# Keys and values of a second cross attention: made during the mix and kept in DRAM

## The chip, the core and the metric

The kernel runs on one core of a Trainium2 chip. The metric is the device time of one execution in microseconds (us), the median over several runs. The profile is one further execution, recorded by the hardware profiler.

## The reference, cut to what matters

Two transformer blocks run one after the other on 512 tokens of width 1024. The second block has a mix of three recurrent branches with gates, an attention over a memory of 256 rows, and a feed-forward network. The keys and values of that attention depend on the memory and on weights alone, not on the tokens.

```python
def second_block(x, mem, ...):
    mem_n = rms_norm_2(mem, norm_mem)
    h = rms_norm_2(x, norm_mix[l])
    p_rw, p_s5, p_gla, p_gate = _split_2(h @ w_in[l], IN_SIZES)
    y_rw, y_s5, y_gla = rwkv7_mix(p_rw, ...), s5_mix(p_s5, ...), gla_mix(p_gla, ...)
    gates = jax.nn.sigmoid(p_gate).reshape(B, L, N_BRANCH, D_MODEL)
    merged = (gates[:, :, 0] * (y_rw @ w_branch[l, 0])
              + gates[:, :, 1] * (y_s5 @ w_branch[l, 1])
              + gates[:, :, 2] * (y_gla @ w_branch[l, 2]))
    x = x + merged @ w_out[l]
    x = x + cross_attention(rms_norm_2(x, norm_xattn[l]), mem_n, xa_wq[l], xa_wkv[l], xa_wo[l])
    x = x + conv_ffn(rms_norm_2(x, norm_ffn[l]), ffn_w_up[l], ...)

def cross_attention(h, mem_n, wq, wkv, wo):          # 4 heads of 256
    q = (h @ wq).reshape(B, L, XA_HEADS, XA_HEAD)
    kv = (mem_n @ wkv).reshape(B, M, 2, XA_HEADS, XA_HEAD)
    k, v = kv[:, :, 0], kv[:, :, 1]
    s = jnp.einsum('bqhd,bkhd->bhqk', q, k) * (XA_HEAD ** -0.5)
    o = jnp.einsum('bhqk,bkhd->bqhd', softmax(s), v).reshape(B, L, D_MODEL)
    return o @ wo
```

## The kernel before, in words

Every matrix product is made of three matmuls, so that two rounded halves of each operand (`hi` and `lo`) stand for one float32 number: high by high (L282), high by low (L283), low by high (L284), in `mm3`. A weight tile of 128x512 (256 KB) is loaded through SP's queue (L310), rounded on ScalarE (L312) and its remainder taken on VectorE (L314); `split` and `split_scaled` do the same for data (L245, L264). A product that is 512 tokens wide issues matmuls of 512 columns, one over the 256 rows of the memory matmuls of 256.

The program is one instruction stream for each engine, in the order in which the Python code emits it. Around a chain of dependent work (a recurrence, an attention) the code emits pieces of other jobs as filler. `kit.push` puts a job (a generator) on a list with a kind; `kit.fill(us)` emits pieces of the jobs that are ready until a counted amount of TensorE work is emitted, kinds 0 and 1 by turns, and within a kind in the order in which they were pushed; `kit.need` emits a job to its end; `kit.flush` emits all that is left. A negative yield in a job says that nothing more of it is due for that long. The filler is thus placed by counted work, not by what happens on the chip.

Buffers of 128x512 come from three tags `a`, `b`, `c`, whose sizes `kit.room` sets. A string of four letters says which tag the streams take: stream 0 the main chain, 1 the jobs of kind 0, 2 the jobs of kind 1, 3 those of kind 2. In the mix it is `"abcc"` with 22, 11 and 21 tiles; `kit.flow(SFLOW)` makes it `"accc"` for the attention.

The second block's part that the change touches, with the times that the profile shows:

- From 1562 to 2111 us the **mix** (`mix`, L2218). The main chain is the rwkv recurrence (`kit.fill(20.0)`, `rwkv`): its preparation (1562 to 1656), the inversion of its small triangular matrices on VectorE (1656 to 1741), then four passes over the chunks (1741 to 1854, 1854 to 1947, 1947 to 2034, 2034 to 2111). The jobs of kind 0 beside it are the low-rank projections (`rwkv_lora`), the gates (`gates_g(b)`, L2182: 192 matmuls of 512 columns, 8 gate tiles each) and the merges of the branches (`merge_g`, L2196). The jobs of kind 1 are the branches S5 and then GLA (`branch1`, `branch2`), of which each pushes its merge and the next gates behind it. `kit.flush` ends it (to 2121).
- 2121 to 2144: `merge_g(0)`, the rwkv branch's output weights, which also makes the operand `O`.
- 2144 to 2198: the product with `w_out` (192 matmuls of 512 columns), with `kit.fill(3, 10)` ahead of each quarter. The filler there is `memory()` (L2253): it loads the memory, splits it and makes its norm (`mr`, `mrb`).
- 2198 to 2362: `cross` (L2281). Head 0's keys and values (`keys`, `vals`) and query are made first, then four heads run in `kit.attention`, which emits 4.5 us of filler at each step: the queries, keys and values of heads 1 to 3 and half of the output product. All keys and values together are 384 matmuls of 256 columns, the queries and the output 384 of 512.
- 2362 to the end: the feed-forward network and the last norm.

Of the kernel before, what the change touches and what calls it, by code (L numbers as in the profile page):

```python
# [10 lines left out]
F32 = mybir.dt.float32  # L11
F32R = mybir.dt.float32r
AF = mybir.ActivationFunctionType
ALU = mybir.AluOpType
# [3 lines left out]
S = 512  # L18
D = 1024
DT = D // 128  # L20
MEM = 256
# [14 lines left out]
BOTH = {"mm": "mm ch si", "si": "si", "ch": "ch"}  # L36
X_BOTH = {"mm": "mm ch", "si": "si", "ch": "mm ch"}
LATE = {"mm": "mm", "si": "si", "ch": "ch", "tr": "ch"}, dict(mm=3, ch=3, si=2)
SFLOW = "accc"
AB_FILL, CD_FILL, X_FILL = (0.9, 1.2), (1.15, 1.3, 1.1), (1.1, 1.4)  # L40


# [607 lines left out]
def tok(b):  # L650
    return lambda a: a[:, b * 128 : b * 128 + 128]
# [3 lines left out]
DENSE_K = [(j * 128, 128, [0, 1, 2, 3]) for j in range(4)]  # L655
# [664 lines left out]
class Second:  # L1320
# [899 lines left out]
    def mix(self):  # L2220
        kit, I = self.kit, self.I
        self.xs = kit.xs
        self.merged, self.gates, self.O = {}, {}, []
        gla, s5 = [], []

        def branch1():
            yield from self.s5_g(s5, lambda: kit.push(branch2(), kind=1))
            kit.push(self.merge_g(1, s5, g1))
            self.g2 = kit.push(self.gates_g(2))

        def branch2():
            yield from self.gla_g(gla)
            kit.push(self.merge_g(2, gla, self.g2))
            self.g0 = kit.push(self.gates_g(0))

        kit.push(branch1(), kind=1)
        lora = kit.push(self.rwkv_lora())
        g1 = kit.push(self.gates_g(1))
        kit.fill(20.0)
        kit.need(lora)  # L2240
        rw = self.rwkv()
        kit.flush()
        kit.run(self.merge_g(0, rw, self.g0))
        job = kit.push(self.memory(), kind=2, stream=1)
        for c in range(4):
            kit.fill(3, 10)
            kit.run(kit.proj_g(I["w_out"][c], self.O, lambda i, p: self.add(2 * c + i, p, "norm_xattn")))
        kit.need(job)


    def memory(self):

        kit, nc, I = self.kit, self.nc, self.I  # L2253
        ms = self.ms = []
        mems = [kit.load("", src=src) for src in I["mem2T"]]
        yield -6
        for m in range(DT):
            if m % 2 == 0:
                mem, hl = mems[m // 2], kit.u()
            c = slice(m % 2 * MEM, m % 2 * MEM + MEM)  # L2260
            ms.append([z[:, c] for z in hl])
            kit.split_scaled(mem[:, c], self.vec("norm_mem", m), *ms[m])
            if m == 0:
                acc = kit.f(MEM)
                nc.scalar.square(acc, mem[:, c])
            else:
                sq = kit.f(MEM)
                nc.scalar.square(sq, mem[:, c])
                nc.gpsimd.tensor_tensor(acc, acc, sq, op=ALU.add)
            yield -1  # L2270
        self.mr = kit.t([128, 2], "mr2", 1)
        nc.vector.tensor_copy(self.mr, kit.rpow(kit.sums(acc, kit.ones, [tok(0), tok(1)]), 1.0 / D, EPS))
        big = kit.spread_begin(self.mr, 2)
        yield -4
        self.mrb = kit.spread_end(big)

    def cross(self):
        kit, nc, I = self.kit, self.nc, self.I
        xs, ms, mr, mrb = kit.xs, self.ms, self.mr, self.mrb
        st, O = {}, {}  # L2280
        sc = kit.small(4, "scq")  # L2281

        def keys(h):
            def emit(j, p):
                if not j:
                    hl = kit.u()
                    st["k", h] = [[z[:, j * MEM : j * MEM + MEM] for z in hl] for j in range(2)]
                f = kit.f(MEM)
                nc.vector.tensor_tensor(f, p, mrb, op=ALU.mult)
                kit.split(f, *st["k", h][j])  # L2290

            yield from kit.proj_g(I["xa_wk"][h], ms, emit)

        def vals(h):
            st["v", h] = []

            def emit(b, p):
                st["v", h].append(kit.u(256))
                kit.split_scaled(p, mr[:, b : b + 1], *st["v", h][b])

            yield from kit.proj_tok_g(I["xa_wv"][h], ms, [tok(0), tok(1)], emit)

        def query(h):
            st["q", h] = []

            def emit(j, p):
                st["q", h].append(kit.u())
                if not h and not j:
                    nc.vector.tensor_scalar(sc, kit.rstd(), 256.0**-0.5, None, op0=ALU.mult)
                kit.split(p, *st["q", h][j])  # L2310

            yield from kit.proj_g(I["xa_wq"][h], xs, emit)

        def out(ts, g=None):
            for t in ts:
                if isinstance(O[t], list):
                    kit.need(O[t])
            for c in range(4):
                w = I["xa_wo"][c][:, :, ts[0] : ts[-1] + 1]
                yield from kit.proj_g(w, [O[t] for t in ts], lambda i, p: self.add(2 * c + i, p, g))  # L2320

        def done(h, sums):
            s = []

            def end():
                big = kit.inverse(sums)
                yield -2
                rb = kit.spread_end(big)
                for j in range(2):
                    nc.vector.tensor_tensor(s[j], s[j], rb, op=ALU.mult)  # L2330
                    hl = kit.u()
                    kit.split(s[j], *hl)
                    O[2 * h + j] = hl

            def f(outs):
                for j in range(2):
                    s.append(kit.f())
                    nc.scalar.copy(s[j], outs[j])
                O[2 * h] = O[2 * h + 1] = kit.push(end(), True)
                if h == 1:  # L2340
                    kit.push(out(range(0, 4)))

            return f

        kit.run(keys(0))
        kit.run(vals(0))
        kit.run(query(0))
        jobs = [[]] + [[kit.push(g(h)) for g in (query, keys, vals)] for h in range(1, 4)]

        def heads():  # L2350
            for h in range(4):
                kit.need(*jobs[h])
                qk = []
                for (qh, ql), (kh, kl) in zip(st["q", h], st["k", h]):
                    qk += [(qh, kh), (qh, kl), (ql, kh)]
                sums = kit.small(4, "sums")
                soft = kit.soft_full(sc, [sums[:, b : b + 1] for b in range(4)])
                yield Head(kit, qk, st["v", h], [(0, 256)] * 4, DENSE_K[:2], soft, done(h, sums), 4.5)

        kit.attention(heads())  # L2360
        kit.flush()
        kit.run(out(range(4, 8), "norm_ffn"))
# [94 lines left out]
def program(tc, ctx, I, out):  # L2457
    kit = Kit(tc, ctx, I)
    f = First(kit)
    kit.banks(*APART)  # L2460
    kit.room("abbb", a=26, b=31)
    V, P = kit.nc.vector, kit.nc.gpsimd
    f.begin()
    kit.by(P)
    f.mixer_ab()
    kit.by(V)
    kit.share(X_BOTH)
    f.cross(0)
    kit.share(BOTH)
    kit.room("aaaa", a=50)  # L2470
    f.ffn(0, f.g_mix[1])
    kit.share(APART[0])
    kit.by(V, P)
    kit.room("abbb", a=24, b=33)
    f.mixer_cd()
    kit.by(V)
    kit.share(X_BOTH)
    f.cross(1)
    kit.banks(*LATE)
    kit.room("abbb", a=31, b=50-31)  # L2480
    s = Second(kit)
    take, done = handover(kit, f, s)
    job = kit.push(s.s5_make_g())
    f.ffn(1, take)
    kit.need(job)
    done()
    kit.room("abcc", a=22, b=11, c=54-22-11)
    s.reset = kit.load("reset")
    s.mix()
    kit.flow(SFLOW)  # L2490
    s.cross()
    kit.room("aaaa", a=50)
    s.ffn()
    s.finish(out)
# [13 lines left out]
```

## Time and profile before

| | |
|---|---|
| median of 3 runs | 2738.64 us (2735.85 to 2743.93) |
| the profiled execution | 2742.08 us, its span in the trace 2740.3 us |
| TensorE matmul busy | 2630.8 us, 96% of the span |
| VectorE, ScalarE, GpSimd busy | 1594.6, 1182.4 and 519.7 us |
| mean granted TensorE clock | 0.968 of full speed |
| HBM read and written | 234.04 and 22.15 MB, 93 GB/s over the span |

The times from 1562 us on are those of the trace, counted from the start of the span. PE is TensorE's matmuls, PEld its weight loads, DVE VectorE, ACT ScalarE, POOL GpSimd, and SP the engine that issues most transfers. A matmul's busy time in the profile is not its pace: matmuls overlap, and the pace is read from the distance of two starts. PEclk is the granted TensorE clock as a share of full speed (2.4 GHz); its other level is one half.

### The profile page before, as it was taken

How to read it: one execution, taken by the hardware profiler on the slowest of the kernel's cores; microseconds unless marked ns; L12 is line 12 of the kernel's file. 1: busy time of each engine (PE TensorE's matmuls, PEld its weight loads, DVE VectorE, ACT ScalarE, POOL GpSimd, SP SyncE). 2: the span in 40 equal slices, each digit the busy share in tenths (PEclk: the TensorE clock that was granted, in tenths of full speed). 3: DMA queues.
4: the chain of work that ended last, by engine and by line, in shares of the span. 5: the costliest groups of instructions: out<-in, count | busy, mean ns of one | idle time of the engine just before them, and what ended most of it. 6: DMA issues, size and time to landing. Idle time of an engine off the chain costs nothing. (4 is left out here: it accounts for less than half of the span.)

```text
span 2740.3 us, 37093 instructions
## 1 busy us (share of the span) xinstructions
PE 2630.8 (96%) x13432; PEld 2124.6 (78%) x13432; DVE 1594.6 (58%) x3076; ACT 1182.4 (43%) x2209; POOL 519.7 (19%) x439
## 2 busy tenths in 40 slices
PE   8999999999999998999999889799999999999998
PEld 6668778888776787887877667677878788888886
DVE  5686654344457867966345667635453656774673
ACT  4576543233445755332333231425223445543443
POOL 5325021011210121243112331111130300100001
PEclk9999999999999999999999998799989999999999
DMA  4112223333422131334434343422212433233332
GB/s 153 36 50 90 61 89 93 100 99 91 128 72 62 55 101 55 116 118 139 142 89 135 108 171 107 108 70 83 66 44 72 119 116 102 81 97 95 100 93 70
DMA packets 172520, 258.51 MB, mean 94 GB/s; under 512 B 42528, under 2 KB 60832, under 8 KB 172320
## 3 DMA queue, kind: packets, MB, share of 16 engines
q1 hardware_dynamic: 172336, 256.13, 30.4%
q8 instruction: 106, 1.74, 0.3%
q14 instruction: 78, 0.64, 0.1%
HBM read 234.04 MB, written 22.15 MB: 93 GB/s over the span
## 5 line engine op out<-in xcount | busy, mean ns | idle before, releaser
L312 ACT CAST wh<-wraw 128x512 fp32r<-128x512 f32 (+1 forms) x777 | 473.4, 613 | 920.9 <-PE ps_mm L283 646.1
L314 DVE TENSOR_TENSOR wl<-wraw,wh 128x512 fp32r<-128x512 f32 (+1 forms) x691 | 488.1, 709 | 346.0 <-ACT wh L312 334.0
L282 PE MATMUL ps_mm<-xs,wh 128*128 128x512 f32 x1544 | 626.7, 406 | 8.9 <-ACT wh L312 7.9
L284 PE MATMUL ps_mm<-xs,wl 128*128 128x512 f32 x1544 | 615.6, 399 | 7.7 <-DVE wl L314 6.9
L283 PE MATMUL ps_mm<-xs,wh 128*128 128x512 f32 x1544 | 616.0, 399 | 2.0 <-DVE xs L264 1.9
L282 PEld LDWEIGHTS ps_mm<-xs,wh 128*128 128x128 f32 x1544 | 295.6, 191 | 76.4 <-ACT wh L312 8.5
L284 PEld LDWEIGHTS ps_mm<-xs,wl 128*128 128x128 f32 x1544 | 295.6, 191 | 75.4 <-DVE wl L314 9.6
L283 PEld LDWEIGHTS ps_mm<-xs,wh 128*128 128x128 f32 x1544 | 295.5, 191 | 66.1 <-DVE xs L264 5.7
L448 POOL TENSOR_TENSOR acc<-acc,za 128x512 f32<-128x512 f32 x59 | 82.0, 1389 | 730.4 <-ACT za L444 729.0
L282 PE MATMUL ps_mm<-za,wh 128*128 128x512 f32 x460 | 183.4, 399 | 5.5 <-ACT za L248 5.5
L284 PE MATMUL ps_mm<-za,wl 128*128 128x512 f32 x460 | 182.0, 396 | 4.1 <-DVE wl L314 4.1
L283 PE MATMUL ps_mm<-za,wh 128*128 128x512 f32 x460 | 180.9, 393 | 0.2 <-DVE za L245 0.2
L314 POOL TENSOR_TENSOR wl<-wraw,wh 128x512 fp32r<-128x512 f32 x86 | 112.4, 1316 | 308.5 <-ACT wh L312 303.7
L1193 POOL TENSOR_TENSOR za<-za,za 128x512 f32<-128x512 f32 x44 | 60.0, 1363 | 461.2 <-ACT za L1192 461.2
L284 PEld LDWEIGHTS ps_mm<-za,wl 128*128 128x128 f32 x460 | 87.3, 190 | 24.8 <-DVE wl L314 4.5
L282 PEld LDWEIGHTS ps_mm<-za,wh 128*128 128x128 f32 x460 | 87.5, 190 | 24.4 <-ACT za L248 6.4
L282 PE MATMUL ps_mm<-zb,wh 128*128 128x512 f32 (+1 forms) x284 | 100.6, 355 | 4.4 <-ACT zb L248 4.4
L245 DVE TENSOR_TENSOR za<-ps_tr,za 128x512 fp32r<-128x512 f32 (+3 forms) x152 | 84.6, 558 | 32.9 <-ACT za L248 31.8
L283 PEld LDWEIGHTS ps_mm<-za,wh 128*128 128x128 f32 x460 | 87.2, 189 | 20.4 <-DVE za L245 1.0
L283 PE MATMUL ps_mm<-zb,wh 128*128 128x512 f32 (+1 forms) x284 | 97.3, 343 | 0.1
L284 PE MATMUL ps_mm<-zb,wl 128*128 128x512 f32 (+1 forms) x284 | 97.3, 343 | 0.0
L468 POOL TENSOR_TENSOR rs<-sm,neghalf 128x4 f32<-128x4 f32 (+2 forms) x32 | 44.9, 1404 | 267.4 <-DVE sm L467 267.4
(592 smaller groups left out, 4918.2 us busy)
## 6 DMA issues: line engine op xcount, KB each, us to landing
wraw<-w_gu SPq DMA_DIRECT2D x176, 256.0 KB, 2.7
wraw<-w_dn SPq DMA_DIRECT2D x96, 256.0 KB, 2.6
wraw<-w_up SPq DMA_DIRECT2D x88, 256.0 KB, 2.6
wraw<-w_gate SPq DMA_DIRECT2D x48, 256.0 KB, 2.7
wraw<-w_dn SPq DMA_DIRECT2D x48, 192.0 KB, 2.3
dram<-za SPq DMA_DIRECT2D x26, 256.0 KB, 2.2
zc<-dram SPq DMA_DIRECT2D x26, 256.0 KB, 4.5
wraw<-w_cd SPq DMA_DIRECT2D x24, 256.0 KB, 2.7
```

The costliest lines, as they stand in the source:

```text
L245: self.nc.vector.tensor_tensor(lo, src, hi.bitcast(F32), op=ALU.subtract)
L282: mm(out, ah, bh, start=start, stop=False, **kw)
L283: mm(out, ah, bl, start=False, stop=False, **kw)
L284: mm(out, al, bh, start=False, stop=stop, **kw)
L312: self.nc.scalar.copy(hl[0], raw)
L314: eng.tensor_tensor(hl[1], raw, hl[0].bitcast(F32), op=ALU.subtract)
L448: self.nc.gpsimd.tensor_tensor(self.acc[0], self.acc[0], sq, op=ALU.add)
L468: self.nc.gpsimd.tensor_tensor(r, ms, self.neghalf[:, :n], op=ALU.pow)
L1193: nc.gpsimd.tensor_tensor(a, a, st["rb"], op=ALU.mult)
```

## The change

`memory()` becomes a job of the mix (kind 2, stream 1), and so does a new job `memory_kv` (kind 0), pushed behind the low-rank projections and ahead of the gates of branch 1. It makes keys and values of all four heads, one head after the other; each head's four tiles (keys and values, `hi` and `lo`) are stored through SP to a scratch in DRAM. Behind `merge_g(0)` the 16 tiles are loaded again, through SP, into tag `b`, and the product with `w_out` has no filler. `cross` makes queries and output alone, with 2.7 us of filler at a step. Tag `b` has 18 tiles in place of 11, and the attention's streams are `"acbc"`.

```diff
-SFLOW = "accc"
+SFLOW = "acbc"
+C_FILL = 2.7
...
         lora = kit.push(self.rwkv_lora())
+        kit.push(self.memory_kv(kit.push(self.memory(), kind=2, stream=1)))
         g1 = kit.push(self.gates_g(1))
...
         kit.run(self.merge_g(0, rw, self.g0))
-        job = kit.push(self.memory(), kind=2, stream=1)
+        kit.flow(SFLOW)
+        self.kv = []
+        for h in range(4):
+            self.kv.append([kit.r(stream=2) for _ in range(4)])
+            for z, d in zip(self.kv[h], self.kv_dram[h]):
+                kit.nc.sync.dma_start(z.bitcast(F32), d)
         for c in range(4):
-            kit.fill(3, 10)
             kit.run(kit.proj_g(I["w_out"][c], self.O, ...))
-        kit.need(job)
...
+    def memory_kv(self, job):
+        kit, nc, I = self.kit, self.nc, self.I
+        self.kv_dram = self.scratch([4, 4, 128, S])
+        kit.need(job)
+        def keys(h):
...
+                nc.vector.tensor_tensor(f, p, self.mrb, op=ALU.mult)
+                kit.split(f, *(z[:, c] for z in hl))
+                if j:
+                    for i, z in enumerate(hl):
+                        nc.sync.dma_start(self.kv_dram[h, i], z.bitcast(F32))
+            return kit.proj_g(I["xa_wk"][h], self.ms, emit)
+        def vals(h):
...
+                kit.split_scaled(p, self.mr[:, b : b + 1], *(z[:, c] for z in hl))
+                if b:
+                    for i, z in enumerate(hl):
+                        nc.sync.dma_start(self.kv_dram[h, 2 + i], z.bitcast(F32))
+            return kit.proj_tok_g(I["xa_wv"][h], self.ms, [tok(0), tok(1)], emit)
+        for h in range(4):
+            yield from keys(h)
+            yield from vals(h)
...
-        kit.run(keys(0))
-        kit.run(vals(0))
         kit.run(query(0))
-        jobs = [[]] + [[kit.push(g(h)) for g in (query, keys, vals)] for h in range(1, 4)]
+        jobs = [[]] + [[kit.push(query(h))] for h in range(1, 4)]
...
-                yield Head(kit, qk, st["v", h], ..., done(h, sums), 4.5)
+                yield Head(kit, qk, st["v", h], ..., done(h, sums), C_FILL)
...
-    kit.room("abcc", a=22, b=11, c=54-22-11)
+    kit.room("abcc", a=22, b=18, c=21)
     s.reset = kit.load("reset")
     s.mix()
-    kit.flow(SFLOW)
     s.cross()
```

How the instructions move is read from the order in which each engine gets them; lines in the changed kernel are one higher from L282 on. The first place is PE in the mix, in the second half of S5, just ahead of the end of the inversion. `ps_si` are S5's outputs, made from `x` and `zc`; `ps_mm<-wh,xs` makes values of GLA from weights and tokens. Before:

```order
L2147 MATMUL ps_si_16006<-x_14957,zc_16064 128x64
L2147 MATMUL ps_si_16007<-x_14957,zc_16064 128x64
L2151 MATMUL ps_si_16006<-zc_15949,zc_16072 128x63
L2151 MATMUL ps_si_16007<-zc_15949,zc_16072 128x63
L2151 MATMUL ps_si_16006<-zc_15952,zc_16074 128x63
L2151 MATMUL ps_si_16007<-zc_15952,zc_16074 128x63
L282 MATMUL ps_mm_16310<-wh_16288,xs_13673 128x256
L283 MATMUL ps_mm_16310<-wl_16289,xs_13673 128x256
L284 MATMUL ps_mm_16310<-wh_16288,xs_13674 128x256
```

and now, where `ps_mm<-zb,wh` makes values of the memory (`zb` its split rows):

```order
L283 MATMUL ps_mm_16299<-zb_14371,wh_16295 128x256
L284 MATMUL ps_mm_16299<-zb_14372,wh_16295 128x256
L285 MATMUL ps_mm_16299<-zb_14371,wl_16296 128x256
L2148 MATMUL ps_si_16263<-x_14895,zc_16310 128x64
L2148 MATMUL ps_si_16264<-x_14895,zc_16310 128x64
L2152 MATMUL ps_si_16263<-zc_16080,zc_16271 128x63
L2152 MATMUL ps_si_16264<-zc_16080,zc_16271 128x63
L2152 MATMUL ps_si_16263<-zc_16083,zc_16273 128x63
L2152 MATMUL ps_si_16264<-zc_16083,zc_16273 128x63
L283 MATMUL ps_mm_16299<-zb_14771,wh_16295 128x256
L284 MATMUL ps_mm_16299<-zb_14772,wh_16295 128x256
L285 MATMUL ps_mm_16299<-zb_14771,wl_16296 128x256
```

S5's last steps had nothing between them; now six matmuls of the memory's values stand between every six of S5's, and what stood in the earlier stretches for `gates_g(1)` comes later.

The second place is VectorE at the end of the mix. L1694 to L1698 finish the rwkv branch (`za`), L245 splits its last tile, L2190 scales a gate, L314 makes a weight's remainder, and L2206 is `merge_g(0)`. Before:

```order
L2190 TENSOR_TENSOR zb_19540<-ps_mm_19491,acc_14154 128x512
L1698 TENSOR_TENSOR za_19447<-ps_ch_19526,za_19447 128x512
L314 TENSOR_TENSOR wl_19646<-wraw_19643,wh_19645 128x512
L245 TENSOR_TENSOR zc_19537<-za_19447,zc_19536 128x512
L2206 TENSOR_TENSOR zb_19028<-ps_mm_19549,zb_19028 128x512
L314 TENSOR_TENSOR wl_19671<-wraw_19668,wh_19670 128x512
L2206 TENSOR_TENSOR zb_19098<-ps_mm_19574,zb_19098 128x512
L245 TENSOR_TENSOR za_19565<-x_16711,za_19564 128x512
L314 TENSOR_TENSOR wl_19696<-wraw_19693,wh_19695 128x512
```

and now:

```order
L2191 TENSOR_TENSOR zb_20044<-ps_mm_19995,acc_14154 128x512
L1699 TENSOR_TENSOR za_19951<-ps_ch_20030,za_19951 128x512
L315 TENSOR_TENSOR wl_20130<-wraw_20127,wh_20129 128x512
L246 TENSOR_TENSOR zc_20041<-za_19951,zc_20040 128x512
L315 TENSOR_TENSOR wl_20136<-wraw_20133,wh_20135 128x512
L2191 TENSOR_TENSOR zb_20084<-ps_mm_20059,acc_14154 128x512
L315 TENSOR_TENSOR wl_20170<-wraw_20167,wh_20169 128x512
L315 TENSOR_TENSOR wl_20176<-wraw_20173,wh_20175 128x512
L2191 TENSOR_TENSOR zb_20124<-ps_mm_20099,acc_14154 128x512
L315 TENSOR_TENSOR wl_20210<-wraw_20207,wh_20209 128x512
L315 TENSOR_TENSOR wl_20216<-wraw_20213,wh_20215 128x512
```

Before, one gate tile of `gates_g(0)` was left beside the chain's end and the merge followed the split at once. Now six of the eight gate tiles of `gates_g(0)`, 144 of its 192 matmuls, stand behind the chain's last tile and ahead of the merge.

The third place is SP's queue around the product with `w_out`. `x<-dram` brings the residual, `zb<-mem2T` the memory, and in the changed kernel `zb<-dram` the kept keys and values. Before:

```order
L310 DMA wraw_19751<-w_out 128x512
L310 DMA wraw_19757<-w_out 128x512
L310 DMA wraw_19797<-w_out 128x512
L188 DMA zb_19743<-mem2T 128x512
L188 DMA zb_19745<-mem2T 128x512
L188 DMA zb_19747<-mem2T 128x512
L310 DMA wraw_19803<-w_out 128x512
L188 DMA zb_19749<-mem2T 128x512
L310 DMA wraw_19850<-w_out 128x512
L1341 DMA x_19788<-dram_14170 128x512
L310 DMA wraw_19856<-w_out 128x512
```

and now:

```order
L2251 DMA zb_20506<-dram_15323 128x512
L2251 DMA zb_20511<-dram_15323 128x512
L1342 DMA x_20556<-dram_14170 128x512
L311 DMA wraw_20571<-w_out 128x512
L1342 DMA x_20602<-dram_14170 128x512
L2251 DMA zb_20512<-dram_15323 128x512
L311 DMA wraw_20612<-w_out 128x512
L311 DMA wraw_20618<-w_out 128x512
L2251 DMA zb_20513<-dram_15323 128x512
L1342 DMA x_20649<-dram_14170 128x512
L311 DMA wraw_20659<-w_out 128x512
L311 DMA wraw_20665<-w_out 128x512
```

The fourth weight tile of `w_out` stood ahead of all but three of the memory's loads; now it is queued behind 13 of the 16 loads of keys and values.

## Rows read from the trace of the kernel before

**Rows 1.** The page's first part: busy time of each engine, share of the span, instructions.

```profile
PE 2630.8 (96%) x13432; PEld 2124.6 (78%) x13432; DVE 1594.6 (58%) x3076; ACT 1182.4 (43%) x2209; POOL 519.7 (19%) x439
```

**Rows 2.** Windows: stretch, length, busy time (instructions) per engine, PEclk, DMA share, GB/s.

```profile
1562.00:1656.00 94.00, 79.28 (x394) 61.91 (x395) 66.13 (x114) 28.39 (x44) 28.15 (x21) 0.84 0.42 142
1656.00:1741.00 85.00, 75.54 (x477) 61.15 (x475) 55.92 (x132) 20.52 (x33) 11.90 (x8) 0.82 0.39 94
1741.00:1854.00 113.00, 105.24 (x669) 83.02 (x668) 58.96 (x103) 41.46 (x73) 21.70 (x19) 0.91 0.31 98
1854.00:1947.00 93.00, 90.04 (x598) 73.00 (x597) 43.07 (x79) 41.92 (x68) 17.69 (x17) 0.98 0.24 73
1947.00:2034.00 87.00, 83.46 (x568) 68.10 (x566) 37.57 (x77) 24.04 (x45) 19.00 (x17) 0.84 0.19 58
2034.00:2111.00 77.00, 75.70 (x511) 60.75 (x510) 34.42 (x67) 24.08 (x43) 13.51 (x12) 1.00 0.20 59
2111.00:2121.00 10.00, 10.00 (x49) 8.04 (x48) 3.81 (x8) 3.68 (x6) 2.06 (x1) 1.00 0.29 92
2121.00:2144.00 23.00, 22.41 (x98) 17.81 (x97) 16.41 (x24) 9.72 (x19) 10.34 (x8) 1.00 0.51 154
2144.00:2198.00 54.00, 48.24 (x199) 38.00 (x199) 31.10 (x44) 25.50 (x46) 16.67 (x15) 0.94 0.36 107
2198.00:2362.00 164.00, 163.82 (x979) 143.76 (x979) 99.72 (x189) 85.12 (x167) 9.92 (x8) 1.00 0.33 102
```

**Rows 3.** Timeline of PE, 2121 and 2236 us: start, duration, instruction, tiles.

```profile
2121.03 0.40 PE L282 MATMUL ps_mm<-zc,wh 128*128 128x512 f32 x1
2121.26 0.40 PE L283 MATMUL ps_mm<-zc,wh 128*128 128x512 f32 x1
...
2236.02 0.28 PE L282 MATMUL ps_mm<-zb,wh 128*128 128x256 f32 x1
2236.14 0.28 PE L283 MATMUL ps_mm<-zb,wh 128*128 128x256 f32 x1
```

**Rows 4.** Timeline of PE around the inversion's end; in brackets the idle time before and its releaser.

```profile
1711.29 1.12 PE L2151 MATMUL ps_si<-zc,zc 64*128 64x63 f32 x8
1715.36 0.55 PE L282 MATMUL ps_mm<-wh,xs 128*128 128x256 f32 x1 [2.95 <-DVE zc L1741]
...
1750.08 1.22 PE L1551 MATMUL ps_ch<-za,za 64*128 64x256 f32 x2 [4.94 <-DVE za L1541]
```

**Rows 5.** Timeline of DVE at the inversion's end.

```profile
1714.54 0.68 DVE L1741 TENSOR_TENSOR zc<-ps_mm,acc 16x512 f32<-16x512 f32 x1
```

**Rows 6.** Groups of DVE instructions, 2198 to 2362: count, busy, mean ns, idle before.

```profile
L314 DVE TENSOR_TENSOR wl<-wraw,wh 128x512 fp32r<-128x512 f32 x64 | 45.1, 707 | 29.6 <-ACT wh L312 29.4
L264 DVE SCALAR_TENSOR_TENSOR zc<-ps_mm,mr,zc 128x256 fp32r<-128x256 f32 x6 | 2.9, 480 | 2.2 <-ACT zc L263 1.7 <-PE ps_si L283 0.5
L2289 DVE TENSOR_TENSOR zc<-ps_mm,zb 128x256 f32<-128x256 f32 x6 | 2.5, 424 | 0.3
L245 DVE TENSOR_TENSOR zc<-zc,zc 128x256 fp32r<-128x256 f32 x6 | 2.5, 417 | 0.0
```

**Rows 7.** Groups of DVE instructions, 1562 to 2121.

```profile
L314 DVE TENSOR_TENSOR wl<-wraw,wh 128x512 fp32r<-128x512 f32 x103 | 78.1, 766 | 34.5 <-ACT wh L312 34.3
L2190 DVE TENSOR_TENSOR zb<-ps_mm,acc 128x512 f32<-128x512 f32 x24 | 16.5, 688 | 41.6 <-PE ps_mm L284 41.4
```

**Rows 8.** DMA issues: count, KB each, median us from issue to landing.

```profile
dram<-zb SPq DMA_DIRECT2D x22, 256.0 KB, 3.5
zc<-dram SPq DMA_DIRECT2D x26, 256.0 KB, 4.5
```

**Rows 9.** Timeline of PE at the start of the product with `w_out`.

```profile
2150.84 0.50 PE L282 MATMUL ps_mm<-za,wh 128*128 128x512 f32 x1 [2.56 <-ACT za L248]
...
2155.28 0.80 PE L282 MATMUL ps_mm<-za,wh 128*128 128x512 f32 x1 [2.98 <-ACT za L248]
```

**Rows 10.** Timeline of POOL, then DVE, at 1747 to 1753 us.

```profile
1747.40 3.16 POOL L1532 TENSOR_TENSOR za<-za,m_own 128x512 f32<-128x512 f32 x2 [15.15 <-DMA za<-dram]
...
1752.71 1.76 DVE L314 TENSOR_TENSOR wl<-wraw,wh 128x512 fp32r<-128x512 f32 x1
```

More of the change, by code (lines that the diff above doesn't have):

```diff
@@ L2254, in memory @@
         ms = self.ms = []
-        mems = [kit.load("", src=src) for src in I["mem2T"]]
-        yield -6
         for m in range(DT):
             if m % 2 == 0:
-                mem, hl = mems[m // 2], kit.u()
+                mem, hl = kit.load("", src=I["mem2T"][m // 2]), kit.u()
+                yield -4
             c = slice(m % 2 * MEM, m % 2 * MEM + MEM)
@@ L2275, in memory, with emit @@
         self.mrb = kit.spread_end(big)
+    def memory_kv(self, job):
[3 more added lines that the diff above has]
+        def keys(h):
+            hl = []
+            def emit(j, p):
+                if not j:
+                    hl[:] = kit.u()
+                c = slice(j * MEM, j * MEM + MEM)
+                f = kit.f(MEM)
+                nc.vector.tensor_tensor(f, p, self.mrb, op=ALU.mult)
[5 more added lines that the diff above has]
+        def vals(h):
+            hl = []
+            def emit(b, p):
+                if not b:
+                    hl[:] = kit.u()
+                c = slice(b * 256, b * 256 + 256)
+                kit.split_scaled(p, self.mr[:, b : b + 1], *(z[:, c] for z in hl))
[6 more added lines that the diff above has]
+            yield from vals(h)
@@ L2277, in cross @@
     def cross(self):
         kit, nc, I = self.kit, self.nc, self.I
-        xs, ms, mr, mrb = kit.xs, self.ms, self.mr, self.mrb
+        xs = kit.xs
         st, O = {}, {}
         sc = kit.small(4, "scq")
[L2283 to L2301, printed above, removed]
+        for h, (kh, kl, vh, vl) in enumerate(self.kv):
+            st["k", h], st["v", h] = ([[z[:, j * MEM : j * MEM + MEM] for z in hl] for j in range(2)] for hl in ((kh, kl), (vh, vl)))
         def query(h):
@@ L2357, in heads @@
                 soft = kit.soft_full(sc, [sums[:, b : b + 1] for b in range(4)])
-                yield Head(kit, qk, st["v", h], [(0, 256)] * 4, DENSE_K[:2], soft, done(h, sums), 4.5)
+                yield Head(kit, qk, st["v", h], [(0, 256)] * 4, DENSE_K[:2], soft, done(h, sums), C_FILL)
         kit.attention(heads())
```

## The prediction

> **What bounds the kernel now.** I read the page's busy shares first, then windows cut at the boundaries of the stages, then the timelines where PE waits. The busy shares say that TensorE is the bound on average, 96% [rows 1]; an average over stages says nothing of what a moved matmul is worth, so the windows come next [rows 2]. The attention (2198 to 2362) is PE alone: 163.82 of 164 us busy at clock 1.00, so a matmul taken out there gives back its pace. The mix before it is not. In its six stretches from 1562 to 2111 PE is idle for 14.7, 9.5, 7.8, 3.0, 3.5 and 1.3 us, 39.8 together, and the clock stands at 0.84, 0.82, 0.91, 0.98, 0.84 and 1.00; length times one less that share is 15.0, 15.3, 10.2, 1.9, 13.9 and 0, 56 us of full-speed work that was not granted. Some 96 us of PE time lie open there, and the change brings 45 us of work to it. The lowest clock is that of the inversion's stretch, where PE stands 2.95 us before the first GLA value and 4.94 us before the first chain product behind it [rows 4], the first ended by a VectorE instruction of the inversion's chain [rows 5]. What the reader should look for is whether the moved matmuls land in such holes.
>
> The pace of a matmul is the distance of two starts: 0.23 us at 512 columns, 0.12 at 256 [rows 3]; I use 0.118, half of 0.236.
>
> **The change, part by part.** Each stretch is its filler (matmuls counted in the order of PE's instructions, times the pace) and a rest, which is chain work, waits and half clock.
>
> *Cross.* 384 matmuls of 256 columns leave: 384 × 0.118 = 45.3 us. As the stretch has no idle time to fall back on, all of it counts, if the softmax stays covered by 2.7 us of filler a step. Near its ends some wait may appear; the nearest rows are two waits of a product for a fresh operand, 2.56 and 2.98 us [rows 9]. Bounds: -45, and -34 if two such pairs (11.1) appear; I take half a pair, 2.8: **-42**.
>
> *Mix, six stretches.* Two heads' keys and values (192 matmuls, 22.7 us) land in 1562–1656 and two in 1656–1741, and gate matmuls that stood there shift to later stretches. Filler before and after, with the rest before in brackets:
> 1562–1656: 204 of 512 columns (46.9 us) become 84 and 192 of 256 (42.0) [47.1];
> 1656–1741: 43.4 becomes 61.4 [41.6];
> 1741–1854: 52.1 becomes 62.3 [60.9];
> 1854–1947: 55.7 becomes 51.1 [37.3];
> 1947–2034: 26.0 becomes 33.9 [61.0];
> 2034–2111: 48.3 becomes 34.0 [28.7].
>
> In the first, VectorE is the busiest engine but PE (66.13 us) and the keys and values ask more of it: eight weight remainders, two scalings, two key splits and two value splits a head, 8 × 0.707 + 2 × 0.424 + 2 × 0.417 + 2 × 0.480 = 8.3 us, 16.6 for two heads [rows 6], against what goes with the 120 gate matmuls that leave, ten remainders (0.766) and five scalings (0.688), 11.1 us [rows 7]: 5.5 more. Bounds -5 (filler alone) and +10; I take **+2**, nearer the middle as both chains share the time.
> In the second, 18.0 us more filler meets 9.5 us idle and 15.3 us of clock: 24.8 us open. Bounds 0 and +18; as filler is placed by counted work and not by holes, some will miss them: **+5**.
> In the third, GLA's chain and the passes wait less when PE is fed: I take the rest of the next stretch (37.3), 62.3 + 37.3 = 99.6 against 113: **-13**. Bounds: the rest stays (+10), or falls to the 28.7 of the densest stretch (-22).
> The fourth loses 4.6 us of filler. With the rest of the densest it would shrink by 13, with that of the fifth (61.0) grow by 19; the clock is already 0.98, so I take **-1**.
> The fifth gains 7.9; the clock of 0.84 leaves 13.9. Bounds +8 (rest kept) and -16 (rest 37.3, filler 33.9); **-3**.
> The sixth loses 14.3 of a dense stretch. Its floor is the chain itself: the stretch before it ran 87 us with 26.0 of filler, so less filler does not shorten a pass without end. Bounds -14 and 0; **-7**.
>
> *The end of the mix.* Because the kind-0 jobs run in order of pushing and the keys come first, 144 of the 192 matmuls of the last gates fall behind the chain's last tile: 30 matmuls become 174, 33 us more at clock 1.00 with nothing to hide them, as `merge_g(0)` needs both. **+33.** That is the price of the change, and it has one answer.
>
> *Product with `w_out`.* Its 192 matmuls are 44.2 of 54 us; the memory's splits leave VectorE, but its two long waits are for `O` [rows 9], not for them. The fourth weight tile is queued on SP behind 13 loads, of which three wait for gate tiles that the merge reads. Three tiles' products end about 2161 in the trace before, 17 us after the merge's end; three loads of 4.5 us [rows 8] and the weight fit. **0**; if the cover were gone, three loads in a row would cost 13.5. The 16 stores (3.5 us each) and 16 loads lie beside stretches at 0.42 of DMA or less, and wait for nobody: nothing, unless a store holds one of 18 tiles, which the fill jobs' order covers with a whole head of matmuls.
>
> Sum: -42 + 2 + 5 - 13 - 1 - 3 - 7 + 33 = **-26**. Against the profiled execution of 2742.08 that is 2716; the median of the runs is 3.4 lower, 2738.64, so **2713**. With the second stretch at 0, the third at -22 and cross at -45 it is 2696, with the second at +18 and the sixth at 0 it is 2733.
>
> **The rivals.**
>
> *A. The chain keeps its length* (22%). Every stretch of the mix takes as long as before: the holes take the filler, but the chain waits for its own engines. For it: in 1562–1741 VectorE, not PE, feeds the chain. Against: the granted clock falls exactly where PE idles. Only +33 and -42 are left: -9, 2730.
>
> *B. All the mix becomes as dense as the sixth stretch* (8%). The rest of each falls to 28.7 and the clock stays at 1.00: 70.7, 90.1, 91.0, 79.8, 62.6 and 62.7 are 457 against 549, -92; VectorE's 66.13 and 5.5 more keep the first from it, and the fifth's chain. I allow two thirds of it, -62, and with -42 and +33: -71, 2668.
> The Trainium skill ("TensorE: Matmul & The Clock Gate", What's actually happening) says that "the default state is throttled, and activity releases the throttle"; by that, filler in the holes would also raise the clock of the chain's own matmuls. The trace agrees as far as it goes, 0.82 beside 9.5 us of idle time and 1.00 beside 1.3 [rows 2].
>
> *C. Slower: VectorE carries the mix* (12%). The place is 1562–1741: the inversion's short instructions queue behind remainders of weights whose matmuls PE does not need so early. The first stretch then grows by 6 (VectorE's 5.5), the second by all 18, and as the passes behind are held by the chain, they keep their lengths: 24 + 33 - 42 = +15, 2754. For it: the two longest waits behind the inversion are VectorE's [rows 4, 5]. Against: VectorE is busy only 55.92 of 85 us. It decides once the six stretches together grow by more than 42 - 33 = 9 us.
>
> *P. VectorE and GpSimd get in each other's way* (8%). One remainder took 1.76 us beside a GpSimd product [rows 10] against the mean of 0.766 in the mix and 0.707 in the attention [rows 6, 7]. Ten such two-operand instructions a head, 40 in all, come where GpSimd is busy 28.15 of 94 and 11.90 of 85 us. At the mean's difference, 0.059, that is 2 us; if one in 4.5 meets a product and loses 1.05, it is 40 × 0.22 × 1.05 = 9 us on the chain: -17, 2722.
> The Trainium skill ("SBUF — State Buffer", SBUF: two separate sides) has the two engines share a port pair as "an exclusive lock", where the later instruction blocks for the whole of the other; by that rule the larger figure would be the likelier. The means in the rows speak for the smaller.
>
> That the change doesn't do what it says is no case here: the order of instructions shows the 384 matmuls in the mix and none in the attention.
>
> **How the numbers follow.** The forecast has 50%, A 22, C 12, B and P 8 each. About 0.3%, 8.2 us, is what a measurement of this kernel can tell from no change: faster is below 2730.4, slower above 2746.9. Faster: 46 of the forecast's 50, half of A (11), B (8) and 7 of P, 72%. Same: 4 of the forecast, 9 of A, 1 of P, 2 of C, 16%. Slower: 10 of C and 2 of A, 12%. The range takes in the forecast's own, 2696 to 2733, A and P, and near half of C: **2692 to 2748**; B, half of C and the forecast's edges, some 18%, lie outside.
>
> **What would show it.** After the change: the attention 122 us long with PE still busy above 97% (if it is 130 or more, the softmax was not covered); a stretch of 40 us between the chain's last tile and `merge_g(0)` filled by gate matmuls at clock 1.00; the stretch that holds the inversion 85 to 95 us long with a clock above 0.82 and shorter waits than 2.95 and 4.94 us; the first pass some 100 us long. The product with `w_out` still about 54 us. The prediction is wrong if the mix up to the chain's end does not shrink by some 15 us (A, C), if it shrinks by 50 (B), or if `w_out` waits for a weight.

## The result, and the profile after

The changed kernel takes 2758.05 us (2754.65 to 2760.65, four runs) against 2737.51 of the kernel before: a ratio of 1.007, 95% interval 1.005 to 1.009. It is 20.5 us slower. The forecast was 2713, the range 2692 to 2748. The nearest case was rival C, 2754, slower through VectorE in the inversion's stretch; it had 12%.

The profiled execution took 2758.22 us, its span is 2756.4 (2740.3 before). First the page's busy shares, which say little, as [rows 1] said little:

```profile
PE 2624.5 (95%) x13432; PEld 2119.6 (77%) x13432; DVE 1588.9 (58%) x3076; ACT 1179.0 (43%) x2208; POOL 524.9 (19%) x439
```

Then windows of the changed kernel, cut at the same places as [rows 2] to within half a microsecond (columns as there: stretch, length, busy times, PEclk, DMA share, GB/s):

```profile
1566.70:1665.50 98.80, 82.99 (x529) 72.06 (x528) 68.13 (x125) 27.83 (x50) 29.69 (x20) 0.82 0.55 178
1665.50:1786.50 121.00, 85.75 (x559) 70.75 (x557) 71.49 (x161) 38.14 (x61) 14.54 (x10) 0.82 0.48 138
1786.50:1889.80 103.30, 98.13 (x626) 76.43 (x625) 51.67 (x90) 35.28 (x66) 15.93 (x13) 1.00 0.28 78
1889.80:1989.30 99.50, 97.16 (x661) 77.43 (x660) 44.84 (x88) 36.36 (x63) 17.12 (x17) 1.00 0.23 74
1989.30:2075.40 86.10, 82.73 (x612) 68.42 (x611) 38.48 (x76) 32.55 (x57) 15.22 (x15) 0.89 0.20 62
2075.40:2141.70 66.30, 65.25 (x473) 53.54 (x473) 36.26 (x69) 20.60 (x39) 24.07 (x19) 0.99 0.15 49
2141.70:2184.00 42.30, 42.30 (x192) 34.72 (x192) 16.98 (x27) 16.22 (x25) 3.36 (x2) 1.00 0.30 87
2184.00:2206.70 22.70, 22.38 (x99) 18.06 (x97) 11.61 (x19) 7.59 (x13) 8.09 (x6) 1.00 0.72 243
2206.70:2257.40 50.70, 46.59 (x192) 36.95 (x193) 24.93 (x37) 20.86 (x34) 12.57 (x9) 0.97 0.45 141
2257.40:2378.10 120.70, 119.89 (x593) 98.84 (x592) 69.52 (x130) 59.75 (x117) 8.45 (x7) 1.00 0.22 70
```

Against [rows 2], the start of the mix's preparation comes 4.7 us later, and the stretches differ by +4.8, **+36.0**, -9.7, +6.5, -0.9, -10.7, +32.3, -0.3, -3.3 and -43.3, which is +16.1 with the start, the difference of the spans. The attention and the end of the mix are as forecast. One stretch is not: the inversion's took 121.0 us where 90 were forecast, and PE is idle there for 35.25 us, against 9.46 before. The open time got larger, not smaller.

Where PE stands in that stretch is read from its timeline (start, duration, instruction; in brackets the idle time before it and its releaser). `ps_mm<-wh,zb` makes values of the memory and `ps_mm<-zb,wh` keys; the text ahead of the prediction calls the latter values.

```profile
1684.64 0.80 PE L283 MATMUL ps_mm<-wh,zb 128*128 128x256 f32 x2 [2.99 <-ACT wh L313]
1705.12 0.58 PE L284 MATMUL ps_mm<-wl,zb 128*128 128x256 f32 x1 [19.68 <-DVE wl L315]
1713.39 0.58 PE L283 MATMUL ps_mm<-zb,wh 128*128 128x256 f32 x1 [5.77 <-ACT wh L313]
```

The 19.68 us end with the remainder of a weight of the memory's values. VectorE's timeline says what it did meanwhile:

```profile
1687.86 1.23 DVE L1505 TENSOR_TENSOR zc<-zc 128x14 f32<-128x14 f32 x1
...
1704.29 0.17 DVE L1506 TENSOR_TENSOR zc<-zc,zc 128x14 f32<-128x14 f32 x1
1704.38 0.69 DVE L315 TENSOR_TENSOR wl<-wraw,wh 128x512 fp32r<-128x512 f32 x1
```

It worked off the inversion: 55 of its short instructions stand back to back in the queue (L1505, L1506 and one memset), and the remainder that PE needs stands behind them, though ScalarE had the weight rounded at 1684.6. Such a block is not new: before, 51 stood back to back, from 1695.85 to 1713.84. But PE had 72 matmuls of 512 columns whose weights were ready, 16.4 us of work without a wait, and then S5's last steps. In its timeline before, the first line is the first of the 72, the second ends the product of GLA's decay, and the third is S5's:

```profile
1683.68 0.39 PE L282 MATMUL ps_mm<-xs,wh 128*16 128x512 f32 x1
...
1689.00 0.40 PE L284 MATMUL ps_mm<-xs,wl 128*16 128x512 f32 x1
...
1700.11 0.55 PE L2147 MATMUL ps_si<-x,zc 128*128 128x64 f32 x4
```

Now PE is fed by matmuls of 256 columns, which use up a weight tile in 1.4 us in place of 2.8 (12 matmuls of 0.118 or 0.23 us), and whose results go through VectorE as well. SP's queue shows a second way of stopping (its waits from 1663 to 1787: total, times, longest):

```profile
SPq L2313 <- ACT zb L264: 31.2, 2, 25.7
SPq L311 <- DVE wl L315: 20.7, 11, 5.2
```

L2313 is the store of a head's values: it heads the queue for 25.7 us, with the next weights (L311) behind it. Here this follows from the first stall, as the values wait for PE's products; what it adds is the 5.77 us that PE stands for the next weight at 1713.39.

### The profile page after: what moved, and what is told of

The parts are those of the page before. It is cut to its first block, busy times and chain, and to the rows that moved or that the text cites. A ratio compares the mean times of both kernels' runs of the same rounds, so it can differ in the third digit from the quotient of the medians.

```text
span 2756.4 us, 37137 instructions
## 1 busy us (share of the span) xinstructions
PE 2624.5 (95%) x13432; PEld 2119.6 (77%) x13432; DVE 1588.9 (58%) x3076; ACT 1179.0 (43%) x2208; POOL 524.9 (19%) x439
## 5 line engine op out<-in xcount | busy, mean ns | idle before, releaser
L315 DVE TENSOR_TENSOR wl<-wraw,wh 128x512 fp32r<-128x512 f32 (+1 forms) x691 | 491.8, 716 | 371.1 <-ACT wh L313 359.3
L315 POOL TENSOR_TENSOR wl<-wraw,wh 128x512 fp32r<-128x512 f32 x86 | 112.4, 1316 | 306.8 <-ACT wh L313 297.1
L283 PE MATMUL ps_mm<-zb,wh 128*128 128x512 f32 (+1 forms) x284 | 103.2, 364 | 10.2 <-ACT wh L313 5.8
L246 DVE TENSOR_TENSOR za<-ps_tr,za 128x512 fp32r<-128x512 f32 (+3 forms) x152 | 84.6, 558 | 32.0 <-ACT za L249 30.9
L284 PEld LDWEIGHTS ps_mm<-za,wh 128*128 128x128 f32 x460 | 87.3, 190 | 20.5 <-DVE za L246 1.0
```

What stands on the lines that cost most here:

```text
L246: self.nc.vector.tensor_tensor(lo, src, hi.bitcast(F32), op=ALU.subtract)
L283: mm(out, ah, bh, start=start, stop=False, **kw)
L284: mm(out, ah, bl, start=False, stop=False, **kw)
L315: eng.tensor_tensor(hl[1], raw, hl[0].bitcast(F32), op=ALU.subtract)
```

## The experiments

Three theories for the stretch were set against each other: **V**, the filler's work on VectorE is queued behind the inversion; **S**, the stores hold up the weight loads in SP's queue; **M**, the order simply puts 18 us more filler there. For all runs the inversion's stretch is cut at the same two instructions (the starts of the last matmul of L1456 and of the first of the second pass, L1482; the edits move the lines), by which it took 84.6 us before and 121.0 in the change. What a run leaves out is said in its expectation.

**few_stores.**

```diff
-                if j:
+                if j and not h:
...
-                if b:
+                if b and not h:
...
-            for z, d in zip(self.kv[h], self.kv_dram[h]):
+            for z, d in zip(self.kv[h], self.kv_dram[0]):
```

> Leaves out 12 of the 16 stores: only head 0's tiles are stored, and all heads load them. In the change the stretch from the end of the preparation to the second pass (the inversion's) took 121.0 us against 84.6 before. Theory S (stores at the head of SP's queue hold the weight loads back; one of them waited 25.7 us): the stretch falls to 95 to 100 us and the time to about 2735. Theory V (the weight remainder is queued on VectorE behind 55 instructions of the inversion): the stretch stays within 5 us of 121 and the time between 2748 and 2760.

Measured: 2763.27 us (1.0097, 1.0081 to 1.0113; the numbers in brackets are the ratio to the kernel before and its 95% interval), the stretch 126.0 us. S alone falls, and V's range for the time is missed by 3 us: without the stores of three heads PE stands even longer, for the remainder:

```profile
1709.21 0.58 PE L285 MATMUL ps_mm<-zb,wl 128*128 128x256 f32 x1 [26.02 <-DVE wl L315]
```

**no_remainder.**

```diff
+        hl_ = getattr(self, 'alone', False)
+        if hl_:
+            hi = self.t([128, CW], 'wh', NW, F32R)[:, :n]
+            self.nc.scalar.copy(hi, raw)
+            return [hi, hi]
...
```

(`alone` is set while the job of keys and values runs.)

> The weights of keys and values have no remainder of their own: the rounded half stands in its place, so 64 instructions leave VectorE, with the same matmuls and loads. Theory V: PE's wait of 19.7 us for that remainder goes, and the inversion's stretch falls from 121 to 95 to 101 us, the time to 2732 to 2740. Theory S: the weight is late on SP, PE waits for ScalarE's rounding instead, and the stretch stays over 112 us. Theory M (18 us more filler in the stretch is all there is): 115 to 121 us.

Measured: 2755.32 us (1.0065, 1.005 to 1.008), the stretch 123.6. No theory has its numbers: the time is above V's range and the stretch above M's. The wait for the remainder is gone, and another, longer by 5.6 us, stands in its place. First PE's timeline, then SP's waits from 1664 to 1712:

```profile
1706.06 0.58 PE L283 MATMUL ps_mm<-zb,wh 128*128 128x256 f32 x1 [25.25 <-ACT wh L315]
```

```profile
SPq L2318 <- DVE zc L1510: 20.2, 1, 20.2
```

L2318 is the store of the values, L1510 an instruction of the inversion (lines are moved by the edit): the store's data are made on VectorE behind the inversion, and the weights that PE waits for are loaded behind the store. S's condition is met, PE waits for ScalarE's rounding, but its store waits in turn for VectorE. So neither V's first path nor S is the cause by itself; each covers the other.

**two_heads.**

```diff
-        for h in range(4):
+        for h in range(2):
             yield from keys(h)
             yield from vals(h)
```

(With `memory()` a second time beside `w_out`, the kept tiles loaded behind `w_out`, heads 2 and 3 in `cross` as before, `C_FILL = 3.6`.)

> Only heads 0 and 1 are made in the mix; the memory is normalised a second time beside w_out, and heads 2 and 3 are made in the attention as before (3.6 us of filler a step). The inversion's stretch then has 264 filler matmuls of 512 columns (60.7 us) in place of 156 and 216 of 256 (61.4): as much filler, half the weight tiles. Theory V: no wait of PE for a remainder over 6 us there, stretch 88 to 102 us; end of the mix 26 us shorter than in the change, attention about 142; in all 2728 to 2745. Theory M: 115 to 121 us there, 2745 to 2755 in all.

Measured: 2761.02 us (1.0087, 1.007 to 1.0104), above the range of either theory, the stretch 112.3, the attention 141.4, the end of the mix 23.8 shorter than in the change. The stretch is 8.7 us better, with 21 remainders on VectorE in place of 32 (two thirds of the weight tiles, not half), but 10 above V's range. The attention (+20.7) and the second and fourth pass (+9.1 and +9.6) take back more than it and the end of the mix give. PE still waits behind the inversion, now for a gate's remainder:

```profile
1722.87 0.79 PE L285 MATMUL ps_mm<-xs,wl 128*128 128x512 f32 x1 [13.83 <-DVE wl L315]
```

The matmuls' width is thus a part of it at most. That it counts whether prepared weights stand ready when the inversion starts is my reading; no run prepared more of them.

**more_fill_in_preparation.**

```diff
-A_FILL, INV_STEP, S5_WAIT, B_MIN, B_FILL = 4.0, 1.7, 35, 1.0, 0.6
+A_FILL, INV_STEP, S5_WAIT, B_MIN, B_FILL = 5.5, 1.7, 35, 1.0, 0.6
```

> The change with 5.5 us of filler in place of 4.0 at each step of the rwkv preparation. The order then leaves 126 in place of 270 matmuls of 512 columns between the last tile of the chain and w_out (33 us less). Theory H (the preparation and the inversion have open PE time): they grow by less than 25 together, and the time is 2735 to 2750. Theory A (a chain keeps its own length and filler adds to it): they grow by all 33 and the time stays 2752 to 2765.

Measured: 2758.75 us (1.0087, 1.006 to 1.0114). What was left behind the chain is gone (32.7 us there, as before the change, where the change has 65.0), but the preparation starts 9.6 us later, takes 11.9 longer, and the inversion's stretch 3.1 more. The time is A's; the preparation and the inversion grew by 15.0 together, which is under H's 25 and far from A's 33, and the rest went into the stretch ahead of them (9.6) and the passes (4.6). In the inversion's stretch 18.5 us more filler than in the change cost only 3.1, as PE's idle time fell from 35.2 to 16.6 us, with no wait over 6.5: there, where 312 of 381 matmuls of filler have 512 columns, filler does cover the stall. Against the kernel before, the stretch has 36.5 us more filler and is 39.5 longer. Over the whole kernel, filler put ahead of the chain costs as much as filler left behind it.

**inversion_emitted_early.**

```diff
-A_FILL, INV_STEP, S5_WAIT, B_MIN, B_FILL = 4.0, 1.7, 35, 1.0, 0.6
+A_FILL, INV_STEP, S5_WAIT, B_MIN, B_FILL = 4.0, 1.0, 35, 1.0, 0.6
```

> The change with the inversion's steps emitted every 1.0 in place of 1.7 counted us: the second pass then stands behind 84 matmuls of 256 columns (9.9 us) in place of 61.4 us of filler, and what is left behind the chain grows from 62 to 86 us. Theory A (filler and chain add up in PE's order wherever the filler stands): the inversion's stretch shrinks by 40 to 60, the passes and the end grow by as much, and the time is 2750 to 2765. Theory M2 (the inversion has its own length, some 65 us with its trips through DRAM, and filler ahead of the second pass only covers it): the stretch and the first pass together take 200 us or more and the time is over 2765.

Measured: 2755.77 us (1.0064, 1.0048 to 1.0079). The stretch and the first pass together take 197.5 us in place of 224.3, and the end of the mix 89.9 in place of 65.0: 27 won, 25 given back. The time is A's again, from the other side, and M2 falls by its time. By itself the stretch shrank by 105, to 16.0, more than the 40 to 60 of A: the second pass began at 1677.2, 38 us before the inversion's last step at 1715.7. So its first matmuls wait for their place in PE's order and not for the inversion. VectorE's stall is not gone: PE stands 20.3 us for a remainder, now in the first pass.

**neither** (the edits of few_stores and no_remainder together).

> Leaves out both 12 of the 16 stores and the weights' remainders. Taken alone each left a stall of 25 us in the inversion's stretch: without stores PE waited 26.0 us for the remainder behind the inversion, without remainders the next weights waited behind a store whose data were behind the inversion. Theory V+S (either path alone is enough to starve PE): with both gone no wait of PE there is over 10 us, the stretch falls from 121 to 95 to 108 us and the time to 2732 to 2745. Theory M (more filler makes the stretch long, the stall only takes other waits' place): 115 us or more, time over 2748.

Measured: 2747.60 us (1.0029, 1.0016 to 1.0041), the stretch 116.0. Some 11 us of the change's loss are gone. That is less than V+S had promised; the stretch is as M said, the time just under M's bound. A third path holds PE for 14.73 us. PE's timeline and ScalarE's show it:

```profile
1710.76 0.58 PE L283 MATMUL ps_mm<-wh,zb 128*128 128x256 f32 x1 [14.73 <-ACT wh L315]
```

```profile
1709.78 0.40 ACT L249 CAST zb<-zb 128x256 fp32r<-128x256 f32 x1 [24.57 <-DVE zb L2300]
1710.10 1.13 ACT L315 CAST wh<-wraw 128x512 fp32r<-128x512 f32 x2
```

L249 rounds a scaled key; the scaling (L2300) is on VectorE behind the inversion, and the next weights' rounding (L315) is behind L249 on ScalarE.

**no_vector_work** (the same, and no instruction of the keys and values on VectorE).

```diff
-                nc.vector.tensor_tensor(f, p, self.mrb, op=ALU.mult)
-                kit.split(f, *(z[:, c] for z in hl))
+                for z in hl:
+                    nc.scalar.copy(z[:, c], p)
...
-                kit.split_scaled(p, self.mr[:, b : b + 1], *(z[:, c] for z in hl))
+                for z in hl:
+                    nc.scalar.copy(z[:, c], p)
```

> As the run without stores and remainders, and the keys and values are written by ScalarE's copies alone (not scaled, no remainders), so that nothing of them needs VectorE. In that run PE still waited 14.7 us, for a weight that ScalarE rounded only after a key copy that waited 24.6 us for VectorE behind the inversion. Theory V (every path of the filler through VectorE stops behind the inversion): no wait of PE over 6 us in the stretch, which falls from 116 to 98 to 106 us (the 85 of before and 18 to 21 of filler), the time to 2728 to 2740. Theory M: stretch 112 or more, 2744 or more.

Measured: 2735.27 us (0.9984, 0.9968 to 1.0), 22.8 us below the change, the stretch 103.4, both in V's ranges. The filler's matmuls are those of the change, but for 15 that moved into this stretch. One wait over 6 us is left, which V had not expected, again a remainder behind the inversion, now of a weight of GLA:

```profile
1707.64 0.61 PE L285 MATMUL ps_mm<-xs,wl 128*16 128x512 f32 x1 [8.50 <-DVE wl L320]
```

That bears out V in its wide form: with the keys' and values' work on VectorE goes the whole loss of the change, 17.6 us of it in this stretch and 5.0 in the preparation. The run takes away load and place in the queue alike; that it is the place is read from the waits, which three queues pass on, and from the last run below. It also shows what is left of M. The stretch has 64.5 us of filler (219 matmuls of 256 columns and 168 of 512) against 43.4 before, 21.1 more, and is 18.8 longer than before: with the stall nearly gone, the filler still adds about its own length. And without any of the keys' and values' work on VectorE the kernel is level with before, not 26 us faster.

**kv_up_front and kv_behind_first_products.** Both make all keys and values in one piece, the first ahead of the rwkv preparation, the second behind its first products.

```diff
-        kit.push(self.memory_kv(kit.push(self.memory(), kind=2, stream=1)))
+        job = kit.push(self.memory(), kind=2, stream=1)
...
         kit.need(lora)
+        kit.run(self.memory_kv(job))
         rw = self.rwkv()
```

```diff
             kit.need(*jobs)
             if t == 0:
+                kit.run(self.memory_kv(self.kvj))
...
-        kit.push(self.memory_kv(kit.push(self.memory(), kind=2, stream=1)))
+        self.kvj = kit.push(self.memory(), kind=2, stream=1)
```

> Keys and values run in one piece ahead of the rwkv preparation; behind them the order of filler is that of the kernel before, stretch by stretch, the attention and w_out that of the change. 45.3 us of matmuls come ahead of the mix, nothing is left behind its chain. Expected by theories V and M alike: the inversion's stretch back to 84 to 88 us, end of the mix 33 us, attention 121, and 2735 to 2745 in all. If the preparation or the passes still differ from before by over 5 us, something besides the filler (the 7 more tiles, the kept tiles' loads) costs time.

Measured: 2746.54 us (1.003, 1.001 to 1.005), 1.5 us above the range; the profiled execution is the fastest of ten, 2739.24 us. The inversion's stretch is 85.1, the end of the mix 32.7, the attention 120.7, but the preparation starts 52.8 us later than before, 7.5 more than the matmuls' 45.3.

> Keys and values in one piece as in the run ahead of the preparation, but behind the first r, k, v products, which cover the memory's norm: there PE was idle 9.7 us ahead of the preparation, against 2.8 before. The 384 matmuls cost 45.3 us there, w_out and the attention give back 46: 2735 to 2743, level with before. If it is over 2748, the place ahead of the preparation costs something of its own.

Measured: 2738.32 us (0.9997, 0.9982 to 1.0012), as expected: level with before, and 20 us faster than the change. The inversion's stretch in the two, beside that of the kernel before, of the change and of the run without work on VectorE (windows, columns as above; in this order: before, the change, no_vector_work, kv_up_front, kv_behind_first_products):

```profile
1656.40:1741.00 84.60, 75.14 (x476) 60.96 (x474) 55.72 (x132) 20.52 (x33) 11.90 (x8) 0.82 0.39 95
```

```profile
1665.50:1786.50 121.00, 85.75 (x559) 70.75 (x557) 71.49 (x161) 38.14 (x61) 14.54 (x10) 0.82 0.48 138
```

```profile
1659.10:1762.50 103.40, 89.13 (x582) 72.91 (x580) 59.51 (x134) 43.80 (x76) 14.70 (x10) 0.90 0.48 135
```

```profile
1704.40:1789.50 85.10, 74.83 (x478) 60.76 (x476) 55.66 (x132) 20.51 (x33) 11.89 (x8) 0.84 0.39 96
```

```profile
1697.30:1782.40 85.10, 74.76 (x476) 60.74 (x474) 55.76 (x132) 20.51 (x33) 11.89 (x8) 0.84 0.39 96
```

The second and the third differ in idle time, 121.00 - 85.75 = 35.3 against 103.40 - 89.13 = 14.3. The last two have before's filler and before's length. The last run does all of the keys' and values' work on VectorE, stores and remainders too, in a place where the inversion does not run: the same load, and the loss is gone. In it the preparation starts 45.5 us later, some 46 us come out of the attention and `w_out`, and 5 and 3 come off the preparation and the first pass, the clock of the preparation being 0.89 in place of 0.84. No run beats the kernel before by more than its interval: where the moved matmuls stood at best, they cost what the attention gave back.

## Why the prediction was wrong

Its steps, one by one, forecast and measured:

| step | forecast | measured |
|---|---|---|
| ahead of 1562 | none | +4.7 |
| preparation, 1562–1656 | +2 | +4.8 |
| inversion, 1656–1741 | +5 (0 to +18) | +36.0 |
| four passes | -13, -1, -3, -7 | -9.7, +6.5, -0.9, -10.7 |
| end of the mix, merge | +33 | +32.0 |
| `w_out` | 0 | -3.3 |
| attention | -42 | -43.3 |

**The step that failed** is the one on the second stretch: "18.0 us more filler meets 9.5 us idle and 15.3 us of clock: 24.8 us open." It took PE's idle time and half clock as room that any matmul could use. None of it was used. Cut at the same instructions, the stretch grew by 36.4 us. Of these, 18.8 stay when the keys' and values' work is off VectorE, at 21.1 us more filler than before: filler adds about its own length, since it stands ahead of the second pass in PE's order. The other 17.6 go with that work: the filler needs VectorE, which first works off 55 instructions of the inversion, and PE's idle time rose by 26 us in place of falling. The prediction had priced the keys' and values' VectorE work, 8.3 us a head, as load on the first stretch, and put nothing for it in the second; what cost was the place in the queue. The bound of +18 was too low for the same reason: it was the filler's own length, as if filler could delay the chain but not be delayed itself.

By the prediction's own sign the mix should have shrunk by some 15 us; its six stretches grew by 26.0. A warning stood in [rows 4] and [rows 5] and was misread: L1741 is no instruction of the inversion, as the prediction has it, but GLA's decay. Its product ended on PE at 1689.4, and it stood behind the inversion's block until 1714.54; PE's 2.95 us were the same kind of wait.

The sum for the passes went wrong too, by a term that it left out: it counted projections as filler, but GLA's own matmuls (`ps_si`) moved as well. The first pass had 96 of them before and has 8 now, the second 3 and 91. This fits that the first became 9.7 us shorter with 10.2 us more filler, and the second 6.5 longer with 4.6 less; no run moved them alone.

**Rival C** had the right place, with the direction of the long wait reversed: I had the inversion wait behind the weights' remainders, and the remainder waited behind the inversion. In the change the inversion's steps ran from 1687.9 to 1719.9, 32 us, against 40 before (1674.0 to 1714.5). Only its four last copies (L1513), which hand the inverse over, came late behind filler in VectorE's queue, at 1790.6 against 1729.8; PE's longest wait in the pass behind them is 0.8 us. That the time came so near to C's 2754 is luck: C had +24 us on the first two stretches and nothing on the passes, and measured are +40.8 and -14.8.

**Rival A** fell as it stands: it kept the length of each stretch, and no hole took the filler for nothing. What held is theory A of the runs, that filler adds its length, and this for the kernel as a whole: moving filler forward (more_fill_in_preparation) or back (inversion_emitted_early) changed the time by 3 us or less. The passes gained 14.8 of the forecast 24 us. What the prediction held against A, that the clock falls exactly where PE idles, is more than [rows 2] say: 0.84 beside 3.5 us idle, 0.98 beside 3.0.

**Rival B** fell. The clock rose in three passes, from 0.91, 0.98 and 0.84 to 1.00, 1.00 and 0.89; in the inversion's stretch it stayed at 0.82, so that the 15.3 us of clock did not come back either. Windows of the change in that stretch (PEclk is the third number from the end):

```profile
1685.00:1705.00 20.00, 0.44 (x2) 0.15 (x1) 17.25 (x60) 0.00 (x0) 3.94 (x3) 0.50 0.00 0
1705.00:1720.00 15.00, 9.00 (x48) 8.28 (x49) 13.68 (x42) 2.78 (x6) 0.00 (x0) 0.56 0.70 225
1720.00:1786.00 66.00, 59.30 (x340) 47.68 (x340) 27.84 (x42) 31.31 (x48) 7.00 (x5) 0.95 0.56 169
```

The clock was at its lower level, one half, while PE stood and for most of the 15 us after, and near full behind that. The Trainium skill ("TensorE: Matmul & The Clock Gate", What's actually happening) has activity release the throttle, as the prediction quotes. The trace agrees as far as it goes: 0.50 beside 0.44 us of work in 20, and 0.95 beside 59.30 in 66.

Part of the moved work ran at the lower level: nine matmuls of 256 columns from 1705.50 to 1707.21 start 0.21 us apart, where the attention before has 0.12. Of 353 distances between two moved matmuls in a row in the first two stretches, 102 are about 0.21 us and 234 are 0.12.

**Rival P** was not tested by a run of its own; the mean remainder in the mix went from 766 ns (103 of them) to 792 (122), 3 us in all, which leaves little for it.

**What was right:** the attention gives back all of its 384 matmuls and the softmax is covered at 2.7 us a step (120.7 us, 0.8 idle); `w_out` does not wait for a weight behind the kept tiles' loads; the gates left behind the chain cost 32.0 us with the merge. Of the 4.7 us ahead of the preparation, 2.4 are there in the first block, at the same instruction and ahead of anything that the change moved; the other 2.3 lie where the memory's norm now stands, and no run took it away.

## What to carry to other kernels

Idle time of an engine is room only for work whose every helper is free then: before moving filler into a stall, look up which engine the stall waits for, and count what the filler needs of that engine, by its place in the queue and not by its load alone. Where a queue is in order, taking one blocked path away only shows the next, so test with all of them away. Here filler placed by counted work ahead of a chain added about its length to it; the sum of what the chain grows by and what is left behind it tells more than either. Count every kind of work that an order moves, the branches' own matmuls too, and not the projections alone.

## What the runs showed of the hardware that was not expected

Three queues, each worked off in order in these traces, passed on one stall of VectorE: VectorE's own (PE stood 19.68 us for a remainder behind the inversion), SP's, where a store that waits for its data kept later loads from being issued (25.25 us of PE's time), and ScalarE's (14.73). Without the stores, or without the remainders, PE still stood 25 us or more at a time; without both it stood 14.73, and without all work of the keys and values on VectorE 8.50.
